# The low parts of the second half of each v table tile are subtracted on POOL

## The chip, the cores and the metric

The kernel runs on one core of one Trainium2 chip. A core has engines that run side by side, each with its own queue of instructions in a fixed order: PE (TensorE, matmuls), DVE (VectorE), ACT (ScalarE), POOL (GpSimd), and SP, whose queue here only issues DMA transfers. They wait for each other through semaphores. The metric is the device time of one execution in microseconds (us), the median over several runs. One execution was also recorded by the hardware profiler; its rows are what "the profile" and "the trace" mean below.

## The reference

One encoder layer over 1024 tokens of width 1024: a token mixer (attention and a two-way Mamba-2 scan, joined by gates), and then a PEER channel mixer. The change lies in the PEER part, which is all that matters here:

```python
def one(xt):                                    # 128 tokens
    q = (xt @ w_query).reshape(T, PEER_HEADS, 2, PEER_D_HALF)
    ...                                         # two top-16 searches per head, then the best 16 pairs
    idx = jnp.take_along_axis(cidx, pos, axis=-1)
    g = jax.nn.softmax(sc, axis=-1)
    u = u_tab[idx]
    a = jax.nn.gelu(jnp.einsum('thkd,td->thk', u, xt).astype(jnp.float32))
    vv = v_tab[idx]
    return jnp.einsum('thk,thkd->td', (g * a).astype(vv.dtype), vv)
```

Each token picks 8 x 16 of 16384 experts; expert e has a row u[e] and a row v[e] of 1024 numbers. All is float32.

## The kernel before, in words

The kernel splits the 1024 tokens for the PEER part. The first 384 are done by **gathering**: for each block of 128 tokens, POOL issues indirect DMAs (line 1192) that fetch one u row per token into a `br` buffer (10 of them), and DVE forms the dot product with the token's vector, which lies in PSUM (line 1224); then rows of v are fetched in the same way, and PE adds them up with small matmuls (line 1271). The other 640 tokens are done **densely**: for each of the 128 tiles of 128 experts PE computes u·x for all tokens (tiles `hb`, from the weight tiles `wh`, `wl`), the gate weights are multiplied in, and PE multiplies with the v tile. Both run at the same time.

Matmuls keep float32 precision by a split: a float32 tile x becomes a high part, cast by ACT to a shorter format (`hi`), and a low part `lo = x - hi`, a subtract; a product is then three matmuls (`mm3`, lines 205 to 207: high·high, low·high, high·low). `split(src, hi, lo, eng)` at line 174 does the cast (line 175) and the subtract (line 176, on the engine given, POOL if none).

The last stage, from some 2540 us to the end, goes through the 128 expert tiles in 43 **groups** of three. Of each group:

- `hidden_parts` (line 1355) gives the activations `a` of one tile of the group by 48 matmuls; those of the other two were computed earlier, and are loaded from DRAM (line 1591).
- `places` (line 1639) loads the group's gate weights into `gt`. There is one `gt` buffer (GTB = 1), so a load waits until the group before has read it.
- `weigh` (line 1594) multiplies `a` by `gt` on DVE (line 1596, "weighing" below), has ACT cast it to `Wh` (line 1599) and DVE subtract for `Wl` (line 1602).
- `vtab(c, u)` (line 1607) loads one half of the v tile into `vr` (three buffers), and splits it into `vh`, `vl`. u = 0 are the first 512 columns, u = 1 the second; both subtracts were given to DVE.
- `mixed` (line 1617) does 144 matmuls: for 8 blocks of columns and 2 halves of the tokens, three tiles by three products, into PSUM tiles named `pb` or `io`, which DVE adds into `acc` (line 1632). Blocks 0 to 3 read the u = 0 tables, blocks 4 to 7 those of u = 1.

The order of work on DVE and POOL in this stage is the order in which the program writes it (line 1637). A list `jobs` holds work to be written between other pieces: after a `mixed` the three `vtab(c, 1)` of the next group to be mixed are put there, and each `weigh` and each `tick` of `hidden_parts` takes one out. Two come out in the weighings of the parked tiles, the third behind the first quarter of the hidden matmuls. Between them `lows` writes the subtracts for the u weights, POOL's `wl` (line 195). The gathers are written by `feed`, paced by estimated engine times, nearly all of them during `mixed`. The order on PE, ACT and SP is set by a scheduler when the kernel is built.

Of the kernel before, what the change touches and what calls it, by code (L numbers as in the profile page):

```python
# [120 lines left out]
def block(ctx, tc, A, out, dbg=None):  # L121
    nc = tc.nc
    dbg = dbg or {}
    V, ACT, PE, POOL = nc.vector, nc.scalar, nc.tensor, nc.gpsimd
# [43 lines left out]
    def f32(t):  # L168
        return t.bitcast(F32)
# [4 lines left out]
    def split(src, hi, lo, eng=None):  # L174
        ACT.copy(hi, src)  # L175
        (eng or POOL).tensor_tensor(lo, src, f32(hi), op=OP.subtract)  # L176
# [204 lines left out]
    for m, o in zip(FIRST, O3):  # L381
        raw = pr.tile([128, S], F32, name="raw", bufs=5)
# [1224 lines left out]
    def vtab(c, u):  # L1607
        raw = d2.tile([128, 4, 128], F32, name="vr", bufs=VB)
        nc.sync.dma_start(raw, A["v"][128 * c:128 * (c + 1), 512 * u:512 * u + 512].rearrange("p (a b) -> p a b", a=4))
        hi = d2.tile([128, 4, 128], FR, name=f"vh{u}", bufs=EG)  # L1610
        lo = d2.tile([128, 4, 128], FR, name=f"vl{u}", bufs=EG)
        split(raw, hi, lo, V)
        T[c, u] = (hi, lo)
        nonlocal at_dma
        at_dma += DLOAD / 2
# [31 lines left out]
    for i, _ in enumerate(park):  # L1647
        tick(part_us, park_dma)
        if parks - 1 - i in groups[0]:
            vtab(parks - 1 - i, 0)  # L1650
    for gi, grp in enumerate(groups):
# [10 lines left out]
        if gi == 0:  # L1662
            w0()
            jobs.extend(lambda c=c: vtab(c, 1) for c in grp)
        else:
            def first(grp=grp):
                jobs.append(lambda: vtab(grp[0], 0))
                w0()

            during = {M0: first}  # L1670
            for k, c in enumerate(grp[1:]):
                during[5 + k] = lambda c=c: vtab(c, 0)
            mixed(groups[gi - 1], during=during)
            jobs.extend(lambda c=c: vtab(c, 1) for c in grp)
# [102 lines left out]
```

## Time and profile before

| what | us |
|---|---|
| median of 3 runs | 4000.57 (3998.97 to 4009.17) |
| the profiled execution, its own time | 4000.45 |
| its span, first to last instruction | 3998.6 |
| PE busy | 3633.1 (91%) |
| DVE busy | 2601.3 (65%) |
| POOL busy | 1828.6 (46%) |
| ACT busy | 1357.6 (34%) |
| DVE subtracts for the v tables, both halves | 198.5 in 256 instructions |

A row of the timeline has the start in us from the span's start, the duration in us, the engine, the line of the kernel, the operation, out<-in by the program's names, the shape, and a count; in brackets stands how long the engine was idle before it and what ended that. A row of a group has the count behind x, then the busy time in us and the mean in ns, then the idle time before and what released it. A row of the waits has who waited for whom, the us in total, the number of times and the longest. A row of the windows has one stretch, with the busy time of each engine. Engine names with a q (SPq) are the queue that issues a transfer, not the transfer.

### The profile page before, as it was taken

How to read it: one execution, taken by the hardware profiler on the slowest of the kernel's cores; microseconds unless marked ns; L12 is line 12 of the kernel's file. 1: busy time of each engine (PE TensorE's matmuls, PEld its weight loads, DVE VectorE, ACT ScalarE, POOL GpSimd, SP SyncE). 2: the span in 40 equal slices, each digit the busy share in tenths (PEclk: the TensorE clock that was granted, in tenths of full speed). 3: DMA queues.
4: the chain of work that ended last, by engine and by line, in shares of the span. 5: the costliest groups of instructions: out<-in, count | busy, mean ns of one | idle time of the engine just before them, and what ended most of it. 6: DMA issues, size and time to landing. Idle time of an engine off the chain costs nothing. (4 is left out here: it accounts for less than half of the span.)

```text
span 3998.6 us, 61125 instructions
## 1 busy us (share of the span) xinstructions
PE 3633.1 (91%) x22927; PEld 3188.4 (80%) x22927; DVE 2601.3 (65%) x5316; ACT 1357.6 (34%) x2658; POOL 1828.6 (46%) x1529
## 2 busy tenths in 40 slices
PE   5799999998898899998888889699999999999998
PEld 3577777776687889996768789697888999788897
DVE  5688851356673578877785467684457898544556
ACT  4265542223333433332226555322222222222222
POOL 3211113555455557777875466444443444444200
PEclk8899999998899999999999899799999999999999
DMA  5111124323366349897777678888887898888732
GB/s 184 37 47 43 54 89 141 103 92 120 96 219 192 119 135 327 310 320 232 248 256 258 226 265 330 326 297 316 317 317 256 299 293 295 300 312 310 246 115 81
DMA packets 386920, 852.08 MB, mean 213 GB/s; under 512 B 32704, under 2 KB 146880, under 8 KB 383808
## 3 DMA queue, kind: packets, MB, share of 16 engines
q1 hardware_dynamic: 276032, 445.47, 33.1%
q0 software_dynamic: 110592, 402.70, 28.8%
q8 instruction: 180, 2.95, 0.3%
q14 instruction: 116, 0.95, 0.1%
HBM read 739.45 MB, written 108.59 MB: 212 GB/s over the span
## 5 line engine op out<-in xcount | busy, mean ns | idle before, releaser
L205 PE MATMUL hb<-ah,wh 128*128 128x320 f32 x2048 | 653.4, 319 | 25.5 <-ACT a L1369 25.5
L207 PE MATMUL hb<-ah,wl 128*128 128x320 f32 x2048 | 641.0, 313 | 9.6 <-issue 9.6
L206 PE MATMUL hb<-al,wh 128*128 128x320 f32 x2048 | 640.1, 313 | 0.0
L1192 POOL DMA_INDIRECT br<-u,bidx x384 | 373.0, 971 | 364.0 <-DVE br L1224 235.4
L195 POOL TENSOR_TENSOR wl<-wr,wh 128x512 fp32r<-128x512 f32 x269 | 352.5, 1316 | 394.6 <-ACT wh L194 364.6
L205 PE MATMUL pb<-Wh,vh 128*128 128x320 f32 x1536 | 476.8, 317 | 55.6 <-ACT Wh L1599 31.7
L176 POOL TENSOR_TENSOR wl<-wr,wh 128x512 fp32r<-128x512 f32 x170 | 232.1, 1369 | 634.9 <-ACT wh L175 455.6
L1192 POOL DMA_INDIRECT br<-v,ixt x384 | 380.0, 990 | 268.4 <-PE gx L1271 154.1
L206 PE MATMUL pb<-Wl,vh 128*128 128x320 f32 x1536 | 480.6, 313 | 2.1 <-DVE Wl L1602 2.1
L207 PE MATMUL pb<-Wh,vl 128*128 128x320 f32 x1536 | 478.7, 312 | 0.6 <-issue 0.6
L1224 DVE SCALAR_TENSOR_TENSOR br<-br,gx 128x1024 f32<-128x1024 f32 x384 | 454.0, 1215 | 8.0 <-DMA br<-u,bidx 5.4
L205 PEld LDWEIGHTS hb<-ah,wh 128*128 128x128 f32 x2048 | 392.5, 192 | 55.2 <-ACT a L1369 29.9
L207 PEld LDWEIGHTS hb<-ah,wl 128*128 128x128 f32 x2048 | 391.5, 191 | 11.0 <-issue 10.9
L206 PEld LDWEIGHTS hb<-al,wh 128*128 128x128 f32 x2048 | 391.9, 191 | 0.0
L1632 DVE TENSOR_TENSOR acc<-acc,pb 128x320 f32<-128x320 f32 x491 | 230.3, 485 | 231.2 <-PE pb L207 170.6
L175 ACT CAST vh<-vr 128x512 fp32r<-128x512 f32 x256 | 151.8, 619 | 636.2 <-PE pb L206 415.5
L205 PEld LDWEIGHTS pb<-Wh,vh 128*128 128x128 f32 x1536 | 289.7, 190 | 84.1 <-ACT Wh L1599 34.9
L194 ACT CAST wh<-wr 128x512 fp32r<-128x512 f32 x288 | 178.3, 619 | 402.5 <-PE hb L206 144.3
L206 PEld LDWEIGHTS pb<-Wl,vh 128*128 128x128 f32 x1536 | 292.4, 190 | 6.3 <-DVE Wl L1602 4.7
L207 PEld LDWEIGHTS pb<-Wh,vl 128*128 128x128 f32 x1536 | 292.6, 190 | 0.4
L1388 DVE TENSOR_TENSOR quad<-io,rig 128x1024 f32<-128x1024 f32 x160 | 191.6, 1221 | 136.7 <-PE pb L1403 77.1
L176 DVE TENSOR_TENSOR vl<-vr,vh 128x512 fp32r<-128x512 f32 x256 | 198.5, 776 | 80.9 <-ACT vh L175 70.0
(362 smaller groups left out, 8266.9 us busy)
## 6 DMA issues: line engine op xcount, KB each, us to landing
wr<-uT SPq DMA_DIRECT2D x256, 256.0 KB
vr<-v SPq DMA_DIRECT2D x256, 256.0 KB
G_d<-stg SPq DMA_DIRECT2D x20, 2048.0 KB
gt<-G_d SPq DMA_DIRECT2D x42, 960.0 KB
a_d<-a SPq DMA_DIRECT2D x85, 320.0 KB
a<-a_d SPq DMA_DIRECT2D x85, 320.0 KB
wr<-wi SPq DMA_DIRECT2D x82, 256.0 KB
sq<-adaT SPq DMA_DIRECT2D x32, 512.0 KB
```

The source lines that it names most:

```text
L175: ACT.copy(hi, src)
L176: (eng or POOL).tensor_tensor(lo, src, f32(hi), op=OP.subtract)
L194: ACT.copy(h, raw)
L195: late.append(lambda: (eng or POOL).tensor_tensor(w, raw, f32(h), op=OP.subtract))
L205: PE.matmul(o, lhsT=wh, rhs=xh, start=first, stop=False)
L206: PE.matmul(o, lhsT=wh, rhs=xl, start=False, stop=False)
L207: PE.matmul(o, lhsT=wl, rhs=xh, start=False, stop=last)
L1192: POOL.indirect_dma_start(out=r, out_offset=None, in_=A[tab], in_offset=bass.IndirectOffsetOnAxis(ap=idx, axis=0))
L1224: V.scalar_tensor_tensor(v2(r), v2(r), 1.0, hrow[0], op0=OP.mult, op1=OP.mult, accum_out=a[:, s:s + 1])
L1388: V.tensor_tensor(x, iota.unsqueeze(1).unsqueeze(1).to_broadcast([128, 2, 4, 128]), ig[:, 0:2, t:t + 4].unsqueeze(3).to_broadcast([128, 2, ...
L1632: V.tensor_tensor(acc[:, m, js], acc[:, m, js], o, op=OP.add)
```

## The change

The subtract of every u = 1 half goes to POOL, that of every u = 0 half stays on DVE:

```diff
         hi = d2.tile([128, 4, 128], FR, name=f"vh{u}", bufs=EG)
         lo = d2.tile([128, 4, 128], FR, name=f"vl{u}", bufs=EG)
-        split(raw, hi, lo, V)
+        split(raw, hi, lo, POOL if u else V)
         T[c, u] = (hi, lo)
```

The casts on ACT, the loads and the estimates that pace the gathers are the same. The order on three engines moves, shown at one group of the last stage, with - for rows that only the kernel before has and + for those that only the changed one has. First POOL, between the gathers of one `mixed` and of the next:

```order
 L1192 DMA br_28733<-u,bidx_7902 128x1024
 L1192 DMA br_28736<-u,bidx_7902 128x1024
+L176 TENSOR_TENSOR vl1_28747<-vr_28744,vh1_28746 128x512
+L176 TENSOR_TENSOR vl1_28760<-vr_28757,vh1_28759 128x512
 L195 TENSOR_TENSOR wl_28507<-wr_28504,wh_28506 128x512
+L176 TENSOR_TENSOR vl1_28784<-vr_28781,vh1_28783 128x512
 L195 TENSOR_TENSOR wl_28803<-wr_28800,wh_28802 128x512
 L1192 DMA br_28882<-u,bidx_7902 128x1024
```

Where two subtracts stood between the gathers, five stand now. The same place on DVE, from a group's second weighing on:

```order
 L1224 SCALAR_TENSOR_TENSOR br_28557,ba_27282<-br_28557,gx_27952 128x1024
 L1596 TENSOR_TENSOR a_28738<-a_28738,gt_28436 128x640
-L176 TENSOR_TENSOR vl1_28747<-vr_28744,vh1_28746 128x512
 L1602 TENSOR_TENSOR Wl_28742<-a_28738,Wh_28741 128x640
 L1596 TENSOR_TENSOR a_28751<-a_28751,gt_28436 128x640
-L176 TENSOR_TENSOR vl1_28760<-vr_28757,vh1_28759 128x512
 L1602 TENSOR_TENSOR Wl_28755<-a_28751,Wh_28754 128x640
-L176 TENSOR_TENSOR vl1_28784<-vr_28781,vh1_28783 128x512
 L1632 TENSOR_TENSOR acc_22555<-acc_22555,io_28837 128x320
```

The three subtracts leave; nothing else moves. SP's queue of loads, before, around the load of the gate weights `gt`:

```order
L186 DMA wr_28800<-uT 128x512
L186 DMA wr_28832<-uT 128x512
L1609 DMA vr_28585<-v 128x512
L1641 DMA gt_28436<-G_d_77 128x10x192
L1609 DMA vr_28670<-v 128x512
L1609 DMA vr_28701<-v 128x512
L1591 DMA a_28738<-a_d_76 128x640
```

and with the change:

```order
L1609 DMA vr_28585<-v 128x512
L1609 DMA vr_28670<-v 128x512
L1609 DMA vr_28701<-v 128x512
L186 DMA wr_28800<-uT 128x512
L186 DMA wr_28832<-uT 128x512
L1641 DMA gt_28436<-G_d_77 128x10x192
L1591 DMA a_28738<-a_d_76 128x640
```

The load of `gt` now stands behind all three v loads and behind the two loads of u weights.

## The prediction

> **What bounds the kernel now.** I read the page first, for the group that the edit touches and its twin on POOL. The same shape costs DVE 776 ns and POOL 1,316 ns (mean):
>
> ```profile
> L195 POOL TENSOR_TENSOR wl<-wr,wh 128x512 fp32r<-128x512 f32 x269 | 352.5, 1316 | 394.6 <-ACT wh L194 364.6
> L176 DVE TENSOR_TENSOR vl<-vr,vh 128x512 fp32r<-128x512 f32 x256 | 198.5, 776 | 80.9 <-ACT vh L175 70.0
> ```
>
> All 256 stand in the last stage, which runs over 43 groups of three v tiles. Next I read that stage by windows. Rows 1 and 3 are groups with u rows gathered and multiplied on DVE (4 and 12 groups, "u groups" below), rows 2 and 4 those with gathered v rows multiplied on PE ("v groups"), row 5 the end without gathers. Behind the length stand the busy us of PE, PEld, DVE, ACT and POOL, the granted clock, the DMA share and GB/s:
>
> ```profile
> 2576.00:2703.00 127.00, 120.19 (x792) 117.35 (x790) 109.17 (x190) 33.88 (x63) 53.85 (x51) 0.99 0.87 294
> 2703.00:3058.00 355.00, 349.88 (x2485) 294.35 (x2484) 175.59 (x300) 80.42 (x150) 153.74 (x148) 1.00 0.85 303
> 3058.00:3441.00 383.00, 353.04 (x2319) 345.49 (x2318) 337.49 (x603) 91.82 (x160) 158.98 (x153) 0.98 0.89 295
> 3441.00:3773.00 332.00, 326.58 (x2314) 271.15 (x2313) 160.37 (x270) 73.25 (x137) 141.63 (x137) 0.99 0.85 300
> 3773.00:3942.00 169.00, 169.00 (x1156) 169.00 (x1155) 100.98 (x178) 43.28 (x75) 11.42 (x8) 1.00 0.39 124
> ```
>
> In the v groups and at the end PE is busy 98 to 100% and DVE half the time: a lighter DVE buys nothing there. In the u groups PE leaves 7 + 30 = 37 us idle and DVE is busy 86 to 88%. Only those 37 us can be won. So the question is what ends DVE's waits in a u group. I took one group (timeline of DVE), from its second weighing to the first of the next:
>
> ```profile
> 3212.80 1.48 DVE L1596 TENSOR_TENSOR a<-a,gt 128x640 f32<-128x640 f32 x1
> 3214.20 0.68 DVE L176 TENSOR_TENSOR vl<-vr,vh 128x512 fp32r<-128x512 f32 x1
> 3215.31 0.83 DVE L1602 TENSOR_TENSOR Wl<-a,Wh 128x640 fp32r<-128x640 f32 x1 [0.43 <-ACT Wh L1599]
> 3216.05 0.82 DVE L1596 TENSOR_TENSOR a<-a,gt 128x640 f32<-128x640 f32 x1
> 3216.79 0.69 DVE L176 TENSOR_TENSOR vl<-vr,vh 128x512 fp32r<-128x512 f32 x1
> 3217.67 0.83 DVE L1602 TENSOR_TENSOR Wl<-a,Wh 128x640 fp32r<-128x640 f32 x1 [0.20 <-ACT Wh L1599]
> 3218.41 0.69 DVE L176 TENSOR_TENSOR vl<-vr,vh 128x512 fp32r<-128x512 f32 x1
> 3219.15 0.49 DVE L1632 TENSOR_TENSOR acc<-acc,io 128x320 f32<-128x320 f32 x1
> ...
> 3225.71 0.83 DVE L1596 TENSOR_TENSOR a<-a,gt 128x640 f32<-128x640 f32 x1 [1.80 <-DMA gt<-G_d]
> ```
>
> The three L176 rows are those that leave DVE. The first two fill pauses in which DVE waits for ACT's Wh in any case. The last row is the point that matters: DVE stands 1.80 us until the gt tile has landed. There is one gt buffer, so its load is issued when the last weighing of the group (3216.05, ending 3216.87) has read it, as SP's queue shows:
>
> ```profile
> 3214.91 0.33 SPq L1609 DMA_DIRECT2D vr<-v  x1
> 3216.90 0.53 SPq L1641 DMA_DIRECT2D gt<-G_d  x1
> ```
>
> The loop of a u group is thus: last weighing, gt load (8.8 us), first weighing, DVE's queue up to the next group. By the waits of the two u windows (first row of each) 4 + 8 = 12 of the 16 groups pause there; and PE waits for what DVE does behind it:
>
> ```profile
> DVE a L1596 <- DMA gt<-G_d: 6.1, 4, 2.8
> ...
> DVE a L1596 <- DMA gt<-G_d: 13.7, 8, 2.6
> PE pb L205 <- DVE acc L1632: 10.2, 8, 2.3
> ```
>
> **The change part by part.** *Removed from DVE*: 128 subtracts. In a gt-bound group their removal gains nothing: what counts is the end of the last weighing, and ahead of it only the row at 3214.20 goes, behind which DVE waits 0.43 us for Wh, whose cast on ACT starts at 3214.55 behind two other casts. In the other 4 groups, where DVE did not pause, 3 x 0.69 = 2.1 us each can go, 8 us in all, if nothing else comes.
>
> *Added to POOL*: three subtracts per group at 1.3 us, and their place decides. By the order of POOL they come right behind the group's last gather, two before the first wl and one before the second. POOL's and ACT's rows for the group:
>
> ```profile
> 3210.07 0.94 POOL L1192 DMA_INDIRECT br<-u,bidx  x1 [1.60 <-DVE br L1224]
> 3211.03 2.56 POOL L195 TENSOR_TENSOR wl<-wr,wh 128x512 fp32r<-128x512 f32 x2
> 3213.75 1.36 POOL L1192 DMA_INDIRECT br<-u,bidx  x1 [0.16 <-issue]
> ...
> 3210.61 0.62 ACT L175 CAST vh<-vr 128x512 fp32r<-128x512 f32 x1 [1.90 <-PE hb L207]
> 3213.51 0.62 ACT L175 CAST vh<-vr 128x512 fp32r<-128x512 f32 x1 [1.76 <-DMA vr<-v]
> 3214.55 0.72 ACT L1599 CAST Wh<-a 128x640 fp32r<-128x640 f32 x1
> ```
>
> The casts are done before POOL comes to each subtract, so two subtracts in a row become five: 3211.03 + 5 x 1.3 = 3217.5 in place of 3213.6. Exactly there DVE runs its weighings, and these cannot run beside a POOL subtract: the row at 3212.80 took 1.48 where its twin at 3216.05 took 0.82, and it ended 0.7 us after POOL's pair did. The dot products (L1224, one input from PSUM) keep their time. How a DVE instruction gets in between POOL's subtracts when these have no gap is seen both ways. Here POOL took turns, its second instruction running 1.88 us and DVE's ending 0.4 us after the first:
>
> ```profile
> 1115.54 1.20 DVE L176 TENSOR_TENSOR bl<-t,bh 128x384 fp32r<-128x384 f32 x1
> ...
> 1115.02 1.30 POOL L176 TENSOR_TENSOR wl<-wr,wh 128x512 fp32r<-128x512 f32 x1
> 1116.28 1.88 POOL L176 TENSOR_TENSOR al<-t,ah 128x640 fp32r<-128x640 f32 x1
> ```
>
> And here, in the same stage as the change, DVE waited through both and ended 0.56 us after them:
>
> ```profile
> 3083.93 3.56 DVE L176 TENSOR_TENSOR vl<-vr,vh 128x512 fp32r<-128x512 f32 x1
> ...
> 3084.43 2.50 POOL L195 TENSOR_TENSOR wl<-wr,wh 128x512 fp32r<-128x512 f32 x2
> ```
>
> Replayed on the group above, in turns: the weighing at 3212.80 gets in after the second subtract, at 3213.6, as today. Wl at 3215.31 waits 0.2 us for POOL's third (pushed to 3215.5) and ends 3216.2. The last weighing then waits for the fourth, until 3217.5, and ends 3218.1: 1.2 us later than 3216.87. If Wl misses its turn once, everything moves one subtract more: +2.5. If DVE waits for the whole train, the first weighing ends 3218.1, and the 2.6 us from its end to that of the last one (3214.28 to 3216.87) put that at 3220.7: +3.8. I take 1.9, between the first two, since the first collision does get in today. In 12 groups this goes into the gt load one for one: 12 x 1.9 = 23 us. In the other 4, DVE's first acc add, now at 3219.15, comes behind the second Wl (1.6 us after the last weighing): 3216.87 + 1.9 + 1.6 = 3220.4, or 1.25 later even without the third subtract: 5 us.
>
> [...]
>
> *SP's queue*: gt now stands behind three v loads and two uT loads, whose buffers POOL frees. In the replay POOL's fifth subtract, pushed twice, ends near 3219, about when the last weighing does: no extra term, but the cover is thin. *Gathers*: the one at 3213.75 starts 4 to 5 us later; the next waits for a DVE row until 3222.25 in any case, and a row is used about ten dots later, over 15 us. Nothing.
>
> *v groups and end*: DVE has slack, but Wl is due soon. In one group the third tile's Wl ends at 2873.32 and PE reads it at 2875.09:
>
> ```profile
> 2867.62 0.82 DVE L1596 TENSOR_TENSOR a<-a,gt 128x640 f32<-128x640 f32 x1
> 2871.92 1.40 DVE L1602 TENSOR_TENSOR Wl<-a,Wh 128x640 fp32r<-128x640 f32 x1 [0.47 <-ACT Wh L1599]
> ...
> 2866.19 1.14 ACT L175 CAST vh<-vr 128x512 fp32r<-128x512 f32 x2 [8.80 <-PE pb L206]
> ...
> 2875.09 0.31 PE L206 MATMUL io<-Wl,vh 128*128 128x320 f32 x1
> ```
>
> In turns the delay stays within these 1.77 us: 0. With a whole train of four from 2866.8 the weighing ends near 2872.7 in place of 2868.4, Wl near 2877.0, 1.9 us too late; eight or so of the 19 v groups have this pattern: 15 us at most. I take 2.
>
> Sum: 23 + 5 + 2 = 30. The profiled execution took 4000.45 us (span 3998.6), the median of the runs is 4000.57, so both give **4030 us**.
>
> **The rivals.** *The whole train blocks*: 12 x 3.8 + 4 x (3.8 - 0.65) = 58, and 15 in the v groups: 4073. For it: the 3.56 us row is the only gapless pair of this very kind in this stage. Against: a gap of 0.16 us let DVE in at 3213.6, and casts that come late leave such gaps. *Faster*: the 4 groups without a pause give up their 8 us, no weighing is held up longer than today since the first collision already exists, and the rest stays: 3992. It decides from the point where the added collisions cost under 0.5 us a group. For it: DVE is busy 88% in the u groups; against: its weighings lie inside the train. *No difference*: the gt load takes over the delay, because fewer transfers run beside it once gathers start later (DMA share 0.89): 8.8 us would have to become about 7: 4000. *That the change does not do what it says* is out: the order shows the instructions moved.
>
> **How the numbers follow.** This forecast (some 4015 to 4047) 0.48, whole train 0.20, no difference 0.18, faster 0.14. A measurement of this kernel tells 0.3% (12 us) from no change; the first two are slower by more: 0.68, 0.18 and 0.14. The range runs from the faster case, 3994, to just short of the whole train, 4068.
>
> **What would show it.** Right: in the u groups POOL runs trains of five; L1596 and L1602 on DVE, whose means in the second u window are now
>
> ```profile
> L1596 DVE TENSOR_TENSOR a<-a,gt 128x640 f32<-128x640 f32 x36 | 34.4, 957 | 14.5 <-DMA gt<-G_d 13.7 <-issue 0.8
> L1602 DVE TENSOR_TENSOR Wl<-a,Wh 128x640 fp32r<-128x640 f32 x36 | 29.7, 826 | 21.6 <-ACT Wh L1599 21.6
> ```
>
> rise to over 1.2 us; the gt load is issued later after the first weighing; u groups lengthen from 30 to 32 us; v groups keep 35 to 36. Wrong: if L1596 and L1602 keep their means, or if the pause before the first weighing shrinks as the delay grows. A gain would show as fewer of the 37 idle us of PE.

## The result

The changed kernel takes 4058.34 us (median of 4 runs, 4049.0 to 4072.75), the kernel before 3999.77 us on the same chip (3998.43 to 4009.17). The ratio is 1.0144 with a 95% interval of 1.0110 to 1.0178: slower by 1.4%, 58 us. The profiled execution of the changed kernel took 4067.01 us (span 4065.2), so its trace shows some 9 us more than the median.

### The profile page after: what moved, and what is told of

Read it like the earlier page. It is cut to its first block, busy times and chain, and to the rows that moved or that the text cites. A ratio compares the mean times of both kernels' runs of the same rounds, so it can differ in the third digit from the quotient of the medians.

```text
span 4065.2 us, 61095 instructions
## 1 busy us (share of the span) xinstructions
PE 3655.1 (90%) x22927; PEld 3205.4 (79%) x22927; DVE 2578.7 (63%) x5188; ACT 1354.9 (33%) x2658; POOL 2029.0 (50%) x1657
## 5 line engine op out<-in xcount | busy, mean ns | idle before, releaser
L176 POOL TENSOR_TENSOR wl<-wr,wh 128x512 fp32r<-128x512 f32 x170 | 231.3, 1365 | 633.5 <-ACT wh L175 464.7
L195 POOL TENSOR_TENSOR wl<-wr,wh 128x512 fp32r<-128x512 f32 x269 | 371.1, 1382 | 152.9 <-ACT wh L194 151.0
L1632 DVE TENSOR_TENSOR acc<-acc,pb 128x320 f32<-128x320 f32 x491 | 230.4, 484 | 244.0 <-PE pb L207 243.1
L176 POOL TENSOR_TENSOR vl<-vr,vh 128x512 fp32r<-128x512 f32 x128 | 190.6, 1500 | 232.1 <-ACT vh L175 228.1
```

The source lines that it names most:

```text
L195: late.append(lambda: (eng or POOL).tensor_tensor(w, raw, f32(h), op=OP.subtract))
L1632: V.tensor_tensor(acc[:, m, js], acc[:, m, js], o, op=OP.add)
```

## The profile after

The 128 subtracts stand on POOL at 1,500 ns each, and the subtracts for `wl`, 1,316 ns before, now take 1,382 (groups of the page):

```profile
L195 POOL TENSOR_TENSOR wl<-wr,wh 128x512 fp32r<-128x512 f32 x269 | 371.1, 1382 | 152.9 <-ACT wh L194 151.0
...
L176 POOL TENSOR_TENSOR vl<-vr,vh 128x512 fp32r<-128x512 f32 x128 | 190.6, 1500 | 232.1 <-ACT vh L175 228.1
```

The windows of the last stage, cut at the same first weighings as before (u groups, v groups, u groups, v groups, end; columns as in the prediction):

```profile
2576.00:2716.00 140.00, 123.37 (x780) 119.75 (x780) 109.66 (x178) 34.23 (x65) 69.85 (x63) 0.94 0.81 266
2716.00:3075.00 359.00, 352.06 (x2493) 295.62 (x2492) 162.81 (x271) 79.09 (x150) 199.10 (x179) 1.00 0.84 299
3075.00:3504.00 429.00, 371.35 (x2342) 358.58 (x2344) 336.90 (x566) 93.03 (x162) 215.69 (x190) 0.94 0.79 264
3504.00:3836.00 332.00, 327.16 (x2285) 271.93 (x2278) 148.62 (x240) 71.43 (x134) 182.36 (x163) 0.98 0.84 298
3836.00:4006.00 170.00, 170.00 (x1163) 170.00 (x1162) 99.92 (x162) 43.33 (x75) 46.45 (x27) 1.00 0.40 125
```

Against 127, 355, 383, 332 and 169 us before, the two u windows are 13 and 46 us longer, the v windows 4 and 0, the end 1. So the loss is 59 us in 16 u groups, 3.7 us each. What grew in the second u window is seen in its groups and then in its waits (who waited for whom, us in total, times, longest):

```profile
L1596 DVE TENSOR_TENSOR a<-a,gt 128x640 f32<-128x640 f32 x36 | 55.7, 1546 | 33.2 <-DMA gt<-G_d 33.1
...
L1602 DVE TENSOR_TENSOR Wl<-a,Wh 128x640 fp32r<-128x640 f32 x36 | 33.6, 932 | 37.5 <-ACT Wh L1599 37.5
```

```profile
DVE a L1596 <- DMA gt<-G_d: 33.1, 8, 8.5
...
PE pb L205 <- DVE acc L1632: 30.3, 8, 7.8
```

The weighings rose from 957 to 1,546 ns, 21 us over 36 of them, and Wl from 826 to 932 ns, 4 us. Beside that the pause for the gate weights rose from 13.7 to 33.1 us, 19 us. These three make 44 of the 46 us of this window.

What a weighing meets is seen in two groups. In the first, POOL runs its five subtracts, and DVE comes to its second weighing 1.8 us after their start (timeline, POOL, then DVE, then SP's queue):

```profile
3243.71 2.55 POOL L176 TENSOR_TENSOR vl<-vr,vh 128x512 fp32r<-128x512 f32 x2
3246.23 1.29 POOL L195 TENSOR_TENSOR wl<-wr,wh 128x512 fp32r<-128x512 f32 x1
3247.49 1.27 POOL L176 TENSOR_TENSOR vl<-vr,vh 128x512 fp32r<-128x512 f32 x1
3248.73 1.25 POOL L195 TENSOR_TENSOR wl<-wr,wh 128x512 fp32r<-128x512 f32 x1
...
3245.48 5.19 DVE L1596 TENSOR_TENSOR a<-a,gt 128x640 f32<-128x640 f32 x1
...
3252.20 0.82 DVE L1596 TENSOR_TENSOR a<-a,gt 128x640 f32<-128x640 f32 x1
...
3245.05 4.07 SPq L1609 DMA_DIRECT2D vr<-v  x3
3249.17 1.17 SPq L186 DMA_DIRECT2D wr<-uT  x2
3253.05 0.53 SPq L1641 DMA_DIRECT2D gt<-G_d  x1
```

The weighing takes 5.19 us and ends 0.7 us after POOL's last subtract: POOL kept it out through four instructions, none of them lengthened. The last weighing comes as much later, and gt is issued behind it, with three v loads and two u loads ahead of it on SP's queue. In the next group the two engines take turns:

```profile
3276.88 2.70 POOL L176 TENSOR_TENSOR vl<-vr,vh 128x512 fp32r<-128x512 f32 x2
3279.54 1.88 POOL L195 TENSOR_TENSOR wl<-wr,wh 128x512 fp32r<-128x512 f32 x1
3281.38 1.91 POOL L176 TENSOR_TENSOR vl<-vr,vh 128x512 fp32r<-128x512 f32 x1
3283.25 1.85 POOL L195 TENSOR_TENSOR wl<-wr,wh 128x512 fp32r<-128x512 f32 x1
...
3278.67 1.60 DVE L1596 TENSOR_TENSOR a<-a,gt 128x640 f32<-128x640 f32 x1
...
3282.07 1.91 DVE L1596 TENSOR_TENSOR a<-a,gt 128x640 f32<-128x640 f32 x1
```

Each weighing waits for one subtract (1.60 and 1.91 us), and three of POOL's run 1.85 to 1.91 us, about 0.6 longer than the 1.25 to 1.29 us above: DVE got in ahead of them. Of the second weighings of the 16 u groups five took 4.8 to 5.2 us, one 2.7; the others took turns or met nothing. So a weighing came in behind one subtract here, and only behind four instructions in the first group.

Over the 14 loops that begin and end in u groups, the means of the pieces are these, worked out from the rows of the weighings and of the gt loads in both traces:

| from ... to | before | after |
|---|---|---|
| last weighing's end to the issue of gt | 0.03 | 0.26 |
| issue of gt to the first weighing | 8.60 | 9.90 |
| first weighing to the second | 17.85 | 17.70 |
| second weighing, its own time | 1.37 | 2.69 |
| its end to the third weighing | 2.45 | 2.85 |
| third weighing, its own time | 0.82 | 1.44 |
| loop | 31.1 | 34.8 |

So 2.2 us of the 3.7 lie in the weighings and the time between them (rows 3 to 6), and 1.5 us in a gt load that is issued later and is in use later after its issue (rows 1 and 2).

## The experiments

Each set of runs has its own runs of the kernel before on the same chip: 4010.79 us for the first four experiments, 4008.97 for the next four, 4010.21 for the last. Ratios are against those.

**Take the subtracts away altogether.**

```diff
-        lo = d2.tile([128, 4, 128], FR, name=f"vl{u}", bufs=EG)
-        split(raw, hi, lo, V)
-        T[c, u] = (hi, lo)
+        if u:
+            ACT.copy(hi, raw)
+            T[c, u] = (hi, hi)
+        else:
+            lo = d2.tile([128, 4, 128], FR, name=f"vl{u}", bufs=EG)
+            split(raw, hi, lo, V)
+            T[c, u] = (hi, lo)
```

> The kernel before, with the subtract of every u = 1 half left out altogether (its matmuls read the high part twice, so the low part of that half is wrong): DVE loses the 128 subtracts and POOL gains none. Theory P (the loss comes from DVE's weighings being locked out by POOL's subtracts): about 3992, since only 4 groups without a pause gain 2.1 us each, and no more than the 37 idle us of PE can go. Rival R (the relief of DVE is worth something in every u group): 16 x 1.9 = 30 us less, 3970.

4011.54 us, ratio 1.0007 (0.9994 to 1.0021). With 128 subtracts gone from DVE and none added to POOL, no gain shows. The relief, which the prediction put at 8 us in four groups, is worth nothing here: the interval ends at a gain of 2 us.

**Keep POOL busy in the same place, without reading.** In place of each subtract POOL writes zeros to the tile three times, so the low part of that half is left out:

```diff
-        split(raw, hi, lo, V)
+        if u:
+            ACT.copy(hi, raw)
+            for _ in range(3):
+                POOL.memset(f32(lo), 0.0)
+        else:
+            split(raw, hi, lo, V)
```

> The changed kernel, with each POOL subtract replaced by three POOL instructions that only write zeros to the same tile (the low part of the u = 1 half is left out): POOL is occupied at the same place for about as long (some 1.5 us each), but reads nothing. Theory P: the weighings are not locked out, 3985 to 4005. Rival Q (POOL's queue is simply longer, and gathers and u weights come late): the loss stays, 4045 to 4065.

4005.44 us, ratio 0.9988 (0.9972 to 1.0005). The groups of the second u window:

```profile
L1615 POOL MEMSET vl<- 128x512 f32 x108 | 56.3, 527 | 7.2 <-PE pb L207 3.0
...
L1596 DVE TENSOR_TENSOR a<-a,gt 128x640 f32<-128x640 f32 x36 | 32.8, 912 | 5.7 <-DMA gt<-G_d 5.7
...
L1602 DVE TENSOR_TENSOR Wl<-a,Wh 128x640 fp32r<-128x640 f32 x36 | 32.3, 897 | 47.1 <-ACT Wh L1599 46.3 <-issue 0.8
```

POOL is held 3 x 527 = 1.6 us per tile, longer than by a subtract, and the weighings do not notice (912 ns, 957 before). So it is not POOL's time that costs, but what its subtracts do to DVE: the 36 weighings of the second u window took 1,546 ns in the mean beside the subtracts of the change, and 912 beside these writes.

**Work on POOL that DVE does not need.** DVE does all subtracts, and POOL repeats the u = 1 ones in four pieces of 128 x 128 into a scratch tile:

```diff
         split(raw, hi, lo, V)
+        if u:
+            for i in range(4):
+                extra = d2.tile([128, 128], FR, name="vx", bufs=1)
+                POOL.tensor_tensor(extra, raw[:, i], f32(hi)[:, i], op=OP.subtract)
```

> The kernel before, all subtracts on DVE, and in addition POOL does the u = 1 subtracts again at the place where the changed kernel has them, into a scratch tile (in four pieces of 128 x 128): the train on POOL without any relief of DVE. Theory P: the loss of the change plus what DVE's three subtracts add now that they meet the train too, 4060 to 4095. If the two parts simply add up, this time less that of the changed kernel is what the relief is worth (8 us by theory P, 30 by rival R).

4179.43 us, ratio 1.0433 (1.0401 to 1.0464): three times the loss of the change, and far more than the 4060 to 4095 us expected. The groups of the second u window, and the timeline of one u group (POOL, DVE, SP's queue), show where it goes:

```profile
L1616 POOL TENSOR_TENSOR vx<-vr,vh 128x128 fp32r<-128x128 f32 x144 | 97.9, 680 | 18.5 <-issue 8.5 <-POOL vx L1616 0.6
...
L1596 DVE TENSOR_TENSOR a<-a,gt 128x640 f32<-128x640 f32 x36 | 34.6, 961 | 89.6 <-DMA gt<-G_d 89.6
```

```profile
3274.06 1.74 POOL L195 TENSOR_TENSOR wl<-wr,wh 128x512 fp32r<-128x512 f32 x1
...
3270.84 1.07 DVE L1596 TENSOR_TENSOR a<-a,gt 128x640 f32<-128x640 f32 x1
...
3287.92 0.83 DVE L1596 TENSOR_TENSOR a<-a,gt 128x640 f32<-128x640 f32 x1 [8.61 <-DMA gt<-G_d]
...
3275.83 0.33 SPq L186 DMA_DIRECT2D wr<-uT  x1
3276.25 0.53 SPq L1645 DMA_DIRECT2D gt<-G_d  x1
```

The weighings hardly wait (961 ns in the mean, beside pieces of 680 ns; the third of this group took 1.07 us). But the last weighing ends at 3271.91 and gt is issued only at 3276.25: on SP's queue it stands behind a u load (3275.83) whose buffer POOL's train, until 3275.80, has to free. This is the queue of which the prediction said that its cover is thin. The runs with another queue, below, test it.

**The other half on POOL.** The second and third u = 0 subtract of a group, written behind the sixth and the seventh block of matmuls, go to POOL, and u = 1 stays on DVE:

```diff
-    def vtab(c, u):
+    def vtab(c, u, eng=V):
...
-        split(raw, hi, lo, V)
+        split(raw, hi, lo, eng)
...
-                during[5 + k] = lambda c=c: vtab(c, 0)
+                during[5 + k] = lambda c=c: vtab(c, 0, POOL)
```

> The kernel before, with another pair moved to POOL: not the u = 1 halves but the second and third u = 0 subtract of each group, which stand between gathers, at a place where DVE runs dot products and acc adds (one input from PSUM). Theory P: no weighing is locked out, and 2 x 0.6 us leave the stretch of DVE between the first and the second weighing, which is in the loop of the u groups: 16 x 1.2 = 19 us less, 3981. Rival Q (POOL's load): two thirds of the loss, 4038.

3995.16 us, ratio 0.9960 (0.9946 to 0.9974): a little faster than before, 16 us where theory P gave 19. Two thirds of the work on POOL (83 subtracts in place of 128) gain at a place beside dot products and adds that read PSUM, where the change loses beside the weighings. In the last stage of this trace 131 adds (L1632) ran beside a subtract on POOL and took 0.48 us, as the others do, and no dot product took more than 1.22 us. The traced execution is the slowest of the ten (4010.49 us), so it does not show where the gain lies.

**Cut the loop through gt.** The gate weights lie in two tiles: `g0` for the tile weighed first, free again right after that, and `gt` for the other two. Once for the kernel before, once for the change (k0 is the place of the first-weighed tile in its group, rest the other two):

```diff
-        gt = d2.tile([128, TA // TBLK, EG, TBLK], F32, name="gt", bufs=GTB)
-        nc.sync.dma_start(gt[:, :, :len(grp)], G_d[:, :, grp[0]:grp[-1] + 1])
+        g0 = d2.tile([128, TA // TBLK, TBLK], F32, name="g0", bufs=GTB)
+        nc.sync.dma_start(g0, G_d[:, :, grp[k0]])
...
+            gt = d2.tile([128, TA // TBLK, EG - 1, TBLK], F32, name="gt", bufs=GTB)
+            nc.sync.dma_start(gt[:, :, :len(rest)], G_d[:, :, grp[rest[0]]:grp[rest[-1]] + 1])
```

> The kernel before, with the gate weights of a group loaded into two buffers instead of one: g0 for the tile that is weighed first, which comes free right after that weighing, and gt for the other two. So the first weighing of the next group no longer waits for the last weighing of this one. Nothing else is edited, though PE's order inside a group comes out otherwise. Theory P (the u groups are bound by the loop last weighing, gt load, first weighing): the pauses of DVE for the gate weights (20 us in the u windows before) go nearly to zero and some of PE's 37 idle us come back: 3975 to 3995 for a before of 4000 to 4011. Rival S (the loop is not what binds; DVE's own queue is): within 0.3% of before. If the smaller pieces make the loads slow, it is slower, and the load's own time must show it.

> The same split of the gate weights, with the u = 1 subtracts on POOL as in the change. What counts is its distance from the split kernel with all subtracts on DVE, beside the 58 us between the change and the kernel before. Theory P (the train of five delays the last weighing, and the gt load carries that delay into the next group): the weighings are still held up (1596 mean near 1.9 us), but the next group's first weighing does not wait for them, so at most half of the 58 us is left, 0 to 29. Rival S (the delay goes through DVE's own queue, or through SP's, whatever the buffers): 45 to 65 us remain.

3997.58 us without the change, ratio 0.9970 (0.9951 to 0.9989), and 4041.36 with it, ratio 1.0079 (1.0062 to 1.0096): 44 us between them in place of 58, which is neither theory's number (up to 29, or 45 to 65). The windows of the two u stretches and the v stretch between them tell more, first without and then with the change:

```profile
2577.00:2704.00 127.00, 121.23 (x800) 118.66 (x799) 109.35 (x192) 34.94 (x65) 55.50 (x53) 0.99 0.90 297
2704.00:3061.00 357.00, 350.99 (x2486) 294.53 (x2485) 175.07 (x298) 80.51 (x150) 153.38 (x149) 1.00 0.85 301
3061.00:3438.00 377.00, 353.91 (x2327) 345.69 (x2329) 339.58 (x605) 91.98 (x162) 158.50 (x153) 0.98 0.91 301
```

```profile
2583.00:2717.00 134.00, 123.84 (x802) 120.44 (x801) 107.54 (x178) 35.79 (x69) 72.94 (x64) 0.96 0.86 283
2717.00:3082.00 365.00, 356.38 (x2487) 297.76 (x2486) 161.69 (x268) 79.55 (x150) 199.51 (x179) 0.99 0.83 294
3082.00:3476.00 394.00, 359.88 (x2321) 348.57 (x2320) 330.04 (x568) 91.26 (x160) 218.02 (x189) 0.97 0.86 286
```

In the u groups the loss is 7 + 17 = 24 us where the change alone has 59. The weighings are still held up,

```profile
L1596 DVE TENSOR_TENSOR a<-a,gt 128x640 f32<-128x640 f32 x24 | 38.2, 1593 | 0.0
...
L1596 DVE TENSOR_TENSOR a<-a,g 128x640 f32<-128x640 f32 x12 | 9.8, 819 | 0.0
```

but no first weighing (second row, from `g0`) waits for gate weights any more. So the loop through gt carries more than half of the loss there. That the v groups lose more in this kernel (8 us in the window shown, 5 in the later one) than in the change (4 and 0) was not expected, and these runs do not say why. Fewer of its second weighings waited through a whole train (two of 16), so the 24 us flatter the cut somewhat.

**The same subtracts, later.** All 128 stay on POOL, but are written one each behind the first three blocks of matmuls, mostly with a gather between them:

```diff
-        split(raw, hi, lo, V)
+        if u:
+            ACT.copy(hi, raw)
+            lows1.append(lambda: POOL.tensor_tensor(lo, raw, f32(hi), op=OP.subtract))
+        else:
+            split(raw, hi, lo, V)
...
             tick(MIX)
+            if lows1:
+                lows1.pop(0)()
```

> The u = 1 subtracts on POOL as in the change, all 128 of the same size, but written later: one each behind the first, second and third block of the following matmuls, with a gather between them, where DVE does dot products with one input from PSUM instead of weighings. Theory P (the cost of the change is the place of the subtracts beside the weighings): the loss goes, -5 to +10 us from before, and the means of 1596 and 1602 are back under 1.0 and 0.95 us. Rival Q2 (any 128 subtracts more on POOL cost that, through gathers that come later or through SP's queue, where loads wait for buffers that POOL frees): 40 to 60 us slower than before.

4047.78 us, ratio 1.0091 (1.0066 to 1.0117): 39 us slower. Theory P misses; the number lies just under the 40 to 60 us of rival Q2, which the interval does not exclude. The trace tells more than the number. Groups and windows (v, u and v groups):

```profile
L1596 DVE TENSOR_TENSOR a<-a,gt 128x640 f32<-128x640 f32 x36 | 41.3, 1146 | 8.3 <-DMA gt<-G_d 8.3
...
L1602 DVE TENSOR_TENSOR Wl<-a,Wh 128x640 fp32r<-128x640 f32 x36 | 41.0, 1138 | 33.8 <-ACT Wh L1599 33.0 <-ACT a L1369 0.8
```

```profile
2717.00:3080.00 363.00, 353.19 (x2488) 296.34 (x2487) 160.52 (x270) 80.85 (x150) 196.12 (x180) 1.00 0.82 297
3080.00:3477.00 397.00, 361.07 (x2323) 349.38 (x2325) 334.38 (x566) 93.23 (x162) 209.13 (x188) 0.97 0.86 285
3477.00:3817.00 340.00, 329.18 (x2305) 271.72 (x2306) 148.25 (x240) 72.39 (x134) 180.45 (x165) 0.98 0.82 293
```

In the second u window 14 us are lost in place of 46, though DVE is still held up: the weighings are 189 ns longer than before, Wl 312 ns, 18 us over the 36 of both. Most of it now hits the last Wl of a group, behind the last weighing, and the gt load does not wait for that. So the subtracts still hold DVE up, which is not the path that rival Q2 gave (late gathers or SP's queue); in the v groups the run does not separate the two. But the v groups, where PE needs Wl soon, lose 8 + 8 us. The subtracts were moved out of one place into another that also has two SBUF inputs; a place that has none was not tried for u = 1.

**Both edits that help.** The split gate weights together with the other half on POOL:

> The split of the gate weights together with the second and third u = 0 subtract of each group on POOL (the u = 1 ones on DVE): the two edits that should help, combined. If their gains add, 0.4% from the moved subtracts and what the split alone brings; if both only fill the same pause of DVE, no more than the better of the two. Theory P says they overlap in part: 3965 to 3990.

3971.09 us, ratio 0.9906 (0.9889 to 0.9923): 38 us faster than before, and the fastest kernel of this study. The two alone gained 11 and 16 us; with intervals of 6 to 8 us either way on each of the three numbers, that 38 is more than their sum is not shown, but the overlap that theory P expected does not show either. In the u windows PE is now idle for 0 and 14 us, in place of 7 and 30:

```profile
2579.00:2695.00 116.00, 115.79 (x787) 115.06 (x786) 103.55 (x182) 34.59 (x64) 64.85 (x60) 1.00 0.96 319
...
3055.00:3416.00 361.00, 347.22 (x2315) 342.18 (x2313) 325.39 (x580) 91.85 (x162) 192.71 (x177) 0.99 0.93 312
```

**Gaps in the train.** The change, with a small write between POOL's subtracts:

```diff
         split(raw, hi, lo, POOL if u else V)
+        if u:
+            POOL.memset(gap, 0.0)
```

> The change, with one addition: POOL writes a small tile (128 x 32, nobody reads it) right behind each of the u = 1 subtracts, so that the train of five is no longer without gaps. Theory G (a weighing that misses its turn at the first hand-over waits to the first gap of POOL, so that gaps in the train end the 4.8 to 5.2 us weighings): no weighing over 3 us in the u groups, mean of 1596 near 1.5 us there, and a gain over the change of 6 x 2.5 = 15 us or more: 4035 to 4045 where the change has 4058 and before 4000 to 4010. Rival N (what let DVE in or kept it out was not the gaps): weighings of 4 to 5 us in some third of the u groups as in the change, 4055 to 4070.

4074.93 us, ratio 1.0164 (1.0147 to 1.0181), not faster than the change, and 5 us above what rival N gave. Five second weighings still took 4.1 to 5.4 us. One of them (timeline, POOL, then DVE):

```profile
3247.28 0.14 POOL L1615 MEMSET gap<- 128x32 f32 x1
3247.36 1.31 POOL L176 TENSOR_TENSOR vl<-vr,vh 128x512 fp32r<-128x512 f32 x1
3248.59 0.14 POOL L1615 MEMSET gap<- 128x32 f32 x1
3248.67 1.30 POOL L195 TENSOR_TENSOR wl<-wr,wh 128x512 fp32r<-128x512 f32 x1
...
3247.82 5.35 DVE L1596 TENSOR_TENSOR a<-a,gt 128x640 f32<-128x640 f32 x1
```

The write of 0.14 us overlaps the end of one subtract and the start of the next, so it moved them apart by some 0.05 us and left no gap between their rows (one subtract ends and the next starts at 3248.67). What is shown is only that such a write did not let DVE in there; whether a real gap would remains open.

**Another queue for gt.** The load of the gate weights is issued from ACT's queue, in the kernel before, in the change, and in the kernel with the repeated subtracts:

```diff
-        nc.sync.dma_start(gt[:, :, :len(grp)], G_d[:, :, grp[0]:grp[-1] + 1])
+        nc.scalar.dma_start(gt[:, :, :len(grp)], G_d[:, :, grp[0]:grp[-1] + 1])
```

> The kernel before, with the loads of the gate weights issued from ACT's queue instead of SP's; there they stand right behind the cast of the last weighing. It is the base for the next two runs. The issue comes some 0.75 us later (behind the cast), 12 groups: +9 us at most by theory P; if the transfer also stands behind others of SP's queue today, it lands sooner, and the two may cancel: 3995 to 4020.

> The change, with the gate weights issued from ACT's queue. In the change the load stands on SP's queue behind three v loads and two u loads, and from its issue to the first weighing it takes 9.9 us where the kernel before has 8.6 (means of 14 u groups). Theory W (the loads ahead of it in the same queue make it land later: 1.5 us of the 3.7 us that a u group loses): from issue to weighing it is back near 8.6, and the loss against the run before this one is some 20 to 25 us less than the change's 58: 30 to 40 us. Rival L (it is later because there is more traffic at that time, whatever the queue): loss 50 to 60 us, and the 9.9 us stay.

> The kernel in which the vector engine does all subtracts and POOL repeats the u = 1 ones in four pieces (4.3% slower than before), with the gate weights issued from ACT's queue. Theory W (its 168 us came from the load of the gate weights, that stood on SP's queue behind loads which wait for POOL's longer train): issue comes within 1 us of the last weighing's end, and most of the loss goes: 4050 to 4095. Rival L (the length of POOL's train and its traffic are the cost): 4150 to 4190.

The first, 4056.29 us, ratio 1.0112 (1.0077 to 1.0147), is itself 46 us slower than before, against an expected 20 at most: the issue comes as early as on SP, but from it to the first weighing it takes 11.0 us (mean of 14) where SP's has 8.6. The packets of the traces go some way to tell why. Until the load's last packet, other transfers moved 0.24 MB per us beside it here, and 0.19 in the kernel before.

Against this base the repeated subtracts cost 4061.27 - 4056.29 = 5 us and the change 4106.06 - 4056.29 = 50 us. The first says that most of the 168 us of the repeated subtracts came from SP's order: 4179.43 - 4061.27 = 118 us go with the queue alone. In the second u window

```profile
3121.00:3617.00 496.00, 387.56 (x2391) 370.73 (x2389) 353.09 (x604) 93.27 (x162) 260.33 (x304) 0.89 0.69 232
```

becomes, with the load on ACT's queue,

```profile
3092.00:3493.00 401.00, 362.18 (x2321) 347.83 (x2323) 352.51 (x603) 93.60 (x162) 254.28 (x297) 0.97 0.80 279
```

with the same train on POOL. The 5 us are a balance: against the base the u windows are 7 + 14 us shorter, and the v windows 15 + 7 longer. From issue to the first weighing this kernel needs 8.0 us (mean of 14), from ACT's queue as well, with 0.10 MB per us of other transfers beside the load. So the queue alone does not make the 11.0 us of the base.

For the change the answer is mixed. By its total it loses nearly as much from either queue (50 us for 58), at the edge of what rival L gave. But the runs of the base are spread over 28 us, and the windows say something else. The second u window of the base and that of the change, both from ACT's queue:

```profile
3078.00:3493.00 415.00, 366.02 (x2345) 358.06 (x2347) 340.64 (x604) 92.52 (x162) 158.60 (x154) 0.93 0.82 273
```

```profile
3097.00:3544.00 447.00, 378.29 (x2359) 364.27 (x2358) 341.40 (x569) 93.73 (x162) 214.65 (x191) 0.94 0.77 254
```

With the first u window (140 and 145 us) the u groups lose 5 + 32 = 37 us where they lost 59 from SP's queue, and the v groups 12 where they lost 4. By the same means over 14 loops the change adds 0.6 us from issue to weighing on ACT's queue (11.0 to 11.6), and 1.3 us, with 0.2 us of a later issue, on SP's; the weighings add 2.2 us on both. So in the u groups some 14 us ((1.5 - 0.6) x 16) to 22 us (59 - 37) go with SP's order of loads, near the 20 to 25 of theory W. As the base has a slower load to begin with, that is an estimate and no clean test. The repeated subtracts show what issuing can cost when the queue's head waits for a buffer: 118 us.

## Why the prediction was right, and where it was short

The sign was right, and so was the place; the 30 us of the forecast were half of the 58. The measured 4058 us lies outside the 4015 to 4047 that the prediction gave as its own case, and nearer to the 4073 of the *whole train* rival than to 4030; it lies inside the range because that was drawn up to just short of this rival. (The range begins at 3994, though the faster case named as its end was worked out as 3992.) By its own steps:

- *What bounds.* Right: 59 us of the loss are in the u groups, 4 in the v groups, 1 at the end.
- *Removed from DVE.* "Nothing" for the gt-bound groups was right. The 8 us for the other four were not there: leaving the subtracts out gave a ratio of 1.0007.
- *Added to POOL.* The train of five came as replayed, and the delay with it. I took 1.9 us per group, between turns (+1.2) and one missed turn (+2.5); the weighings lost 2.2 us in the mean, a mixture of these cases and of the whole train (+3.8), for which five of the 16 groups waited. That the 1.9 came near the mean is thus partly luck, and the *whole train* rival came true in a third of the groups.
- *Into the gt load "one for one".* This is the step that failed. The sum kept the load at its 8.8 us, and the no-difference rival had it shrink to 7. The time from the last weighing's end to the first weighing grew from 8.6 to 10.2 us, 1.5 us in each of 16 groups, 24 us that stand nowhere in the sum. With the weighings' 16 x 2.2 = 35 us in place of 28 that makes the 59. Why the load lands later is settled only in part: in two of the 14 loops it was issued 1.6 to 1.7 us late behind a u load on SP's queue, and on ACT's queue 0.6 us of the 1.5 are left. The amount of traffic does not explain the rest: until the load's last packet, 7.95 us after its issue before and 9.07 with the change (means of 14), other transfers moved 0.19 and 0.20 MB per us beside it. More of it were gathered rows, 1.26 MB in place of 0.84; no run isolates what that does.
- *The other four groups.* Priced at 1.25 us each. In four of the 14 loops the first weighing (at 2671.47, 3102.28, 3134.03 and 3286.49) did not wait for gt before; from first weighing to first weighing they grew by 3.6, 1.8, 3.9 and 2.8 us, 3.0 in the mean. In three of them DVE now waits 2.1 to 3.2 us for gt: once the weighings came late, they were bound by gt like the rest.
- *SP's queue.* "No extra term" was short by some 14 to 22 us, by the estimate from the runs with ACT's queue, and these are part of the 24 above. "The cover is thin" was right: with the longer train of the repeated subtracts the order of the same queue cost 118 us (4179 us, and 4061 from ACT's queue).
- *v groups and end.* 2 us forecast, some 5 found (4 + 0 + 1).
- *What would show it.* The weighings' mean passed 1.2 us (1,546 ns); Wl's did not (932 ns): the last one of each u group came behind the train and in most groups kept its 0.82 us. The u groups went to 34.8 us, not 32. The pause before the first weighing did not shrink, but more than doubled.

POOL's time in that place costs nothing (the write-only run, ratio 0.9988), and the relief of DVE gives nothing (the left-out run, 1.0007). So the loss comes from subtracts that keep DVE out. That it then passes through the weighings and the later gt load is read from the loops, and borne out by the split run and the later train in the u groups; the extra loss of both in the v groups is not explained.

## What to carry to other kernels

Before moving a two-input elementwise operation to POOL, look at what DVE does beside it: next to DVE operations with two SBUF inputs it can keep DVE out through a whole train (5.19 us in place of 0.82), next to operations that read PSUM it did not slow them here (the adds kept 0.48 us, the dot products at most 1.22), and moving two thirds as many subtracts there gained 0.4%. Where a single buffer closes a loop, a delay ahead of its release comes back with the load behind it, and that load must be priced again and not kept at its old duration (here it took 9.90 us from its issue to the first weighing in place of 8.60). And a load that waits for a buffer which POOL frees held up the load behind it on its queue: 118 us in one of these kernels.

## What the runs showed of the hardware

- A DVE instruction with two SBUF inputs that came while POOL was in a subtract, with the next one following without a gap, mostly got in after the first. Where it did not, it waited through up to four, 5 us and more. In the last stage of twelve traces (both kernels, and all experiments but the left-out and the write-only run) this longer wait struck 26 of 69 weighings that stood directly behind a dot product, and 7 of some 870 other instructions that came in such a place. What decides it is not known.
- The granted clock was lower where PE waited more: in the second u window it was 0.98 before, 0.94 with the change and 0.89 with the repeated subtracts, and PE's busy time rose from 353 to 371 us for 1% more matmuls. The table of the loop shows no trace of it between the first and the second weighing (17.85 and 17.70 us), so nothing here says that it was a cause of the loss; no run isolates it.
- The last packet of the same 960 KB load, issued right behind the last weighing (means of 14), came 7.95 us after its issue from SP's queue in the kernel before and 10.35 us from ACT's, but 6.19 us from ACT's with the repeated subtracts and 6.35 us from SP's in the write-only run. Until then the other transfers moved 0.19, 0.24, 0.10 and 0.10 MB per us beside it: in these four kernels the time went with the traffic, and not with the queue. In the change it took 9.07 us at 0.20, so traffic is not all of it.
